# A decoder layer on eight cores: the norm factor moved to PSUM, the conv diagonals loaded instead of built, and the last tiles reordered

## Chip, cores, metric

One Trainium2 chip, eight cores; each core takes one of the eight sequences and they do not exchange data. The metric is the device time of the slowest core in microseconds (us). Most executions of a kernel agree within 0.3%. Some fall into a slower state, in which one die shows a lower clock.

Engine names in the profile: PE is TensorE (matmuls), PEld its weight loads, DVE VectorE, ACT ScalarE, POOL GpSimd, SP SyncE. SBUF is the on-chip working memory; PSUM is the small memory into which PE writes its results.

## The reference, cut

```python
def reference(x, ...):                       # x: (8, 2048, 1024)
    h = rmsnorm(x, g_mix_norm)
    proj = h @ w_in + b_in                   # q | k | v | glu | two gates
    y_attn = sliding_window_attention(q, k, v, sinks) @ w_attn_proj   # window 128
    y_conv = conformer_conv(glu_in) @ w_conv_proj + b_conv_proj       # GLU, depthwise conv 31, LayerNorm, silu
    x = x + (gate0 * y_attn + gate1 * y_conv) @ w_out
    h2 = rmsnorm(x, g_ffn_norm)
    x = x + (silu(gate) * up) @ w_ffn_down   # d_ff 2816
    return rmsnorm(x, g_final)
```

## The kernel before

The tokens of a core are treated in four groups of 512, features on the 128 partitions. A norm has four steps. Squares are formed; PE multiplies them by a matrix of 1/1024 into one PSUM bank (the statistic, already the same on all partitions); ScalarE turns that into the factor `exp(-0.5 * ln(mean + eps))`; VectorE multiplies eight tiles by gain and factor.

```python
def rstd(stat, tg):                          # norm factor of token group tg
    b = tg % 2
    act(nb.rs[:, b, :], ps[stat][:, :], AF.Ln, ..., bias=epsb)
    act(nb.rs[:, b, :], nb.rs[:, b, :], AF.Exp, ..., scale=-0.5)      # factor in SBUF

def norm_out(tg, src, c, g):                 # eight of these per group: "the body's multiplies"
    stt_("dve", hT[:, c, tsl(tg)], src[:, c, :], g[:, c:c + 1], nb.rs[:, b, :], ALU.mult, ALU.mult, ...)

def build_diag(c):                           # 16 GpSimd multiplies in all: diagonal conv weights
    for G in range(4 * c, 4 * c + 4):
        tt_("pool", wS[:, G, :, :], emask..., wcol[:, G, :]..., ALU.mult, ...)
...
for i in range(2, NTT):                      # the main loop of the first part, one step per 128 tokens
    if i < 6:
        build_diag(i - 2)
    ...
    scores(n); glu_b(tg, c); attn_t(n - 2); pv(n - 1); glu_a(tg, c)
    run(mid.get(i, ()))                      # squares, statistics, norm multiplies of later groups
    ...
    run(end.get(i, ()))
    if i in (5, 9):                          # the long steps: the q, k, v projection of group 2 or 3
        p1_qk(g, (4, 0, 1)); ...             # its matmuls read hT, which norm_out writes
```

`attn_t` issues four transposes at once on PE, once per step. They have a source line of their own, so they serve as milestones: transposes 0 to 15.

In the long step, `end` also forms the squares of group 3, and GpSimd adds them in pairs (four additions of 128x512), while VectorE multiplies group 2. At the end of the kernel the last group is treated in two halves of 256 tokens: down projection, residual addition, squares, statistics, factor, eight output multiplies, writes.

The softmax here doesn't subtract the row's maximum and nothing guards it: scores larger than these inputs give would overflow.

## Time and profile before

Median 904.51 us of six runs. The first view is the page of the slowest core (core 6): its span, busy times, the engines on the chain of work that ended last, and the group of VectorE multiplies (source line, engine, operation, output<-input, shape, count | busy us, mean ns | idle time before and who ended it).

```profile
span 902.1 us, 14231 instructions; the slowest of 8 cores (899.8 to 902.1 us)
PE 869.1 (96%) x4778; PEld 401.1 (44%) x4778; DVE 398.3 (44%) x641; ACT 323.5 (36%) x468; POOL 153.3 (17%) x173
PE 86%; DVE 3%; DMA 3%; issue 3%; POOL 2%; ACT 2%; DVEq 0%; POOLq 0%; ACTq 0%; SPq 0%
L411 DVE SCALAR_TENSOR_TENSOR arena<-arena 128x512 bf16<-128x512 f32 (+2 forms) x158 | 123.1, 814 | 115.9 <-ACT arena L398 109.0
```

PE is busy nearly always; every other engine is at or under 44%. Only what PE waits for can be gained. The next view is the same core in stretches (us from the start, length, then busy us and instruction counts by engine, clock, share of the DMA engines, GB/s).

```profile
84.00:108.00 24.00, 19.13 (x107) 8.05 (x105) 14.59 (x19) 16.17 (x23) 11.17 (x10) 0.86 0.24 57
130.00:828.00 698.00, 697.87 (x3681) 316.19 (x3672) 292.19 (x449) 212.45 (x308) 78.37 (x93) 1.00 0.31 59
880.00:902.10 22.10, 10.84 (x94) 8.71 (x92) 14.43 (x27) 9.07 (x19) 4.96 (x5) 0.84 0.52 191
```

From 130 to 828 us PE hardly ever waits (697.87 of 698 us busy). The losses are early and at the very end. The worst is the long step; here is its timeline on core 6 (start, length, engine, line, operation, count, and in brackets the idle time before it and who ended that).

```profile
83.44 0.39 PE L725 MATMUL ps<-arena 128*128 128x128 bf16 x4
...
88.52 1.02 PE L395 MATMUL ps<-arena 128*128 128x512 bf16 x4 [0.86 <-ACT arena L398]
89.06 8.72 DVE L411 SCALAR_TENSOR_TENSOR arena<-arena 128x512 bf16<-128x512 f32 x7 [0.74 <-ACT arena L398]
90.04 6.52 POOL L401 TENSOR_TENSOR arena<-arena 128x512 bf16<-128x512 f32 x4 [1.25 <-ACT arena L398]
90.56 0.81 PE L395 MATMUL ps<-arena 128*128 128x512 bf16 x3 [1.02 <-DVE arena L411]
92.23 0.89 PE L395 MATMUL ps<-arena 128*128 128x512 bf16 x3 [0.87 <-DVE arena L411]
...
108.19 0.39 PE L725 MATMUL ps<-arena 128*128 128x128 bf16 x4
```

Between transposes 5 (83.44) and 6 (108.19) PE gets three matmuls each time VectorE finishes a multiply, and waits again. Seven multiplies take 8.72 us, beside four GpSimd additions in 6.52 us (1.66 us each in the groups by form). (The step holds matmuls for 38,416 columns. The trace's matmuls of 512 columns start 0.216 us apart, which gives 16.2 us for the step; this is the "about 16" of the prediction below.) PE's waits in total, 40 to 130 us on the same core (who waited <- for whom: us, times, longest):

```profile
PE ps L395 <- DVE arena L411: 4.9, 6, 1.8
PE ps L395 <- ACT arena L398: 3.5, 8, 0.9
```

The tail, same core, from its last statistics matmuls on:

```profile
894.17 0.38 PE L395 MATMUL ps<-arena 128*128 128x256 bf16 x2 [1.80 <-ACT arena L398]
894.65 0.47 ACT L398 ACTIVATE arena<-ps,arena 128x256 f32<-128x256 f32 x1 [0.22 <-PE ps L395]
895.21 0.81 ACT L398 ACTIVATE arena<-arena 128x256 f32<-128x256 f32 x2
895.73 2.93 DVE L411 SCALAR_TENSOR_TENSOR arena<-arena 128x256 f32<-128x256 f32 x6 [1.24 <-ACT arena L398]
898.69 0.72 POOL L401 TENSOR_TENSOR arena<-arena 128x256 f32<-128x256 f32 x1 [1.50 <-ACT arena L398]
```

Ln starts 0.1 us after the last matmul; then come Exp and six multiplies on VectorE; GpSimd comes last. The span ends at 902.1, when the last write is known to have landed.

### The profile page before, as it was taken

To read this page: it belongs to the slowest core of one execution; us is meant where nothing else is said; L and a number is where in the kernel's file an instruction comes from. 1 tells how busy PE (TensorE), PEld (TensorE's weight loads), DVE (VectorE), ACT (ScalarE), POOL (GpSimd) and SP (SyncE) were. 2 spreads that over 40 slices of the span, in tenths; PEclk is the share of its full clock that TensorE was granted. 3 is DMA by queue.
4 is the path that set the end of the run, shared out by engine and by line. 5 is a ranking of instruction groups with operands and counts; after the bars stand their busy time and mean duration, and the time that the engine had idled before them with its cause. 6 is when DMAs were issued, how large, how long until landed. Compare 5 with 4: busy or idle time off the path is not lost.

```text
span 902.1 us, 14231 instructions; the slowest of 8 cores (899.8 to 902.1 us)
## 1 busy us (share of the span) xinstructions
PE 869.1 (96%) x4778; PEld 401.1 (44%) x4778; DVE 398.3 (44%) x641; ACT 323.5 (36%) x468; POOL 153.3 (17%) x173
## 2 busy tenths in 40 slices
PE   7788899999999999999999999999999999999995
PEld 4343345444444444444444444444444444444443
DVE  2257562666574334467411353121452125435346
ACT  3567656765663343243411100111001110024454
POOL 2148333321311000122000000000000000012222
PEclk9899899999999999999999999999999999999998
DMA  8750316363239632500521340212501125002115
GB/s 189 215 141 1 82 34 114 80 132 93 67 128 138 120 54 41 186 1 2 94 37 34 53 65 1 47 24 47 82 1 24 30 41 83 0 1 85 45 60 187
DMA packets 27910, 64.47 MB, mean 71 GB/s; under 512 B 3520, under 2 KB 14016, under 8 KB 27072
## 3 DMA queue, kind: packets, MB, share of 16 engines
q0 software_dynamic: 9696, 29.36, 20.2%
q1 hardware_dynamic: 17456, 33.57, 12.0%
q8 instruction: 41, 0.67, 0.3%
q10 hardware_dynamic: 688, 0.63, 0.3%
q14 instruction: 29, 0.24, 0.1%
HBM read 75.67 MB, written 8.39 MB: 93 GB/s over the span
## 4 chain that ended last, share of the span: by engine, by line
PE 86%; DVE 3%; DMA 3%; issue 3%; POOL 2%; ACT 2%; DVEq 0%; POOLq 0%; ACTq 0%; SPq 0%
PE ps L395 86%; DVE arena L411 2%; ACT arena L398 1%; POOL arena L401 1%; DMA arena<-w_qkv 1%; DMA arena<-x 1%; DMA arena<-w_glu 1%; DVE arena L401 1%; POOL arena L694 0%; PE ps L725 0%; ACT L398 0%; POOL arena L689 0%; DVE arena L716 0%; DVEq L1149 0%; SPq L388 0%
## 5 line engine op out<-in xcount | busy, mean ns | idle before, releaser
L395 PE MATMUL ps<-arena 128*128 128x512 bf16 (+5 forms) x4714 | 867.3, 364 | 24.7 <-ACT arena L398 8.7
L395 PEld LDWEIGHTS ps<-arena 128*128 128x128 bf16 (+2 forms) x4714 | 396.8, 98 | 489.0 <-issue 65.7
L401 DVE TENSOR_TENSOR arena<-arena,ps 128x512 f32<-128x512 f32 (+1 forms) x216 | 147.8, 687 | 292.3 <-PE ps L395 277.4
L398 ACT ACTIVATE arena<-ps 128x512 f32<-128x512 f32 (+1 forms) x150 | 87.8, 596 | 342.3 <-PE ps L395 336.3
L411 DVE SCALAR_TENSOR_TENSOR arena<-arena 128x512 bf16<-128x512 f32 (+2 forms) x158 | 123.1, 814 | 115.9 <-ACT arena L398 109.0
L398 ACT ACTIVATE arena<-ps,arena 128x512 f32<-128x512 f32 (+2 forms) x193 | 127.1, 683 | 123.7 <-PE ps L395 122.6
L398 ACT ACTIVATE arena<-arena 128x512 f32<-128x512 f32 (+6 forms) x98 | 78.7, 819 | 87.4 <-DVE arena L411 42.8
L401 POOL TENSOR_TENSOR arena<-arena 128x512 bf16<-128x512 f32 (+3 forms) x54 | 60.7, 1128 | 200.8 <-ACT arena L398 190.8
L388 POOL DMA_DIRECT2D arena<-w_ffn_in x22 | 11.7, 533 | 347.2 <-PE ps L395 347.2
L401 DVE TENSOR_TENSOR arena<-arena 128x512 f32<-128x512 f32 (+3 forms) x75 | 53.1, 737 | 8.6 <-ACT arena L398 3.3
L398 ACT ACT_TABLE_LOAD x27 | 34.6, 1283 | 21.7 <-PE ps L395 11.1
L401 DVE TENSOR_TENSOR arena<-ps,arena 128x256 bf16<-128x256 f32 (+3 forms) x72 | 22.6, 333 | 28.3 <-PE ps L395 24.3
L411 DVE SCALAR_TENSOR_TENSOR arena<-arena,ps 128x512 f32<-128x512 f32 x32 | 21.9, 685 | 18.2 <-ACT arena L398 16.8
L411 DVE SCALAR_TENSOR_TENSOR arena<-ps,arena 128x512 f32<-128x512 f32 x32 | 21.7, 685 | 17.2 <-PE ps L395 17.2
L689 POOL TENSOR_SCALAR_AFFINE_SELECT arena<-arena 128x1024 bf16<-128x1024 bf16 x16 | 18.6, 1165 | 51.2 <-ACT arena L398 51.2
L407 POOL TENSOR_SCALAR arena<-arena 128x512 f32<-128x512 f32 x16 | 15.6, 983 | 56.6 <-ACT arena L398 55.5
L694 POOL TENSOR_SCALAR_AFFINE_SELECT arena<-arena 128x1024 bf16<-128x1024 bf16 x15 | 18.3, 1222 | 0.7
L753 POOL CAST arena<-arena 128x512 bf16<-128x512 f32 x16 | 12.2, 766 | 34.6 <-ACT arena L398 25.9
L729 DVE COPY arena<-ps 128x512 bf16<-128x512 bf16 x16 | 6.7, 419 | 15.3 <-PE ps L725 15.3
L388 POOL DMA_DIRECT2D arena<-w_mix x8 | 4.4, 556 | 25.6 <-PE ps L395 25.3
L716 DVE RECIPROCAL arena<-arena 128x4 f32<-128x4 f32 x32 | 5.7, 178 | 3.3
L725 PE MATMUL ps<-arena 128*128 128x128 bf16 x64 | 6.2, 219 | 0.7 <-ACT arena L398 0.7
(18 smaller groups left out, 20.9 us busy)
## 6 DMA issues: line engine op xcount, KB each, us to landing
arena<-x SPq DMA_DIRECT2D x32, 512.0 KB, 6.8
arena<-w_ffn_in POOLq DMA_DIRECT2D x22, 512.0 KB, 5.3
arena<-arena SPq DMA_DIRECT2D x128, 67.5 KB, 2.0
arena<-w_mix POOLq DMA_DIRECT2D x8, 768.0 KB, 13.0
out<-arena SPq DMA_DIRECT2D x6, 1024.0 KB, 3.9
arena<-w_ffn_down POOLq DMA_DIRECT2D x2, 1536.0 KB, 15.0
arena<-w_ffn_down POOLq DMA_DIRECT2D x2, 1280.0 KB, 13.6
arena<-w_glu POOLq DMA_DIRECT2D x4, 512.0 KB, 9.9
```

Of the source, the lines that this page charges most:

```text
L388: return S.add(eng, lambda e: e.dma_start(out=out, in_=in_, **kw), r=r, w=w, dma=True)
L395: return op("pe", lambda e: e.matmul(out=out, lhsT=lhsT, rhs=rhs, start=start, stop=stop, **kw), r, w)
L398: return op("act", lambda e: e.activation(out=out, in_=in_, func=func, **kw), r, w)
L401: return op(eng, lambda e: e.tensor_tensor(out=out, in0=in0, in1=in1, op=alu), r, w)
L407: return op(eng, lambda e: e.tensor_scalar(out=out, in0=in0, scalar1=s1, scalar2=s2, op0=op0, op1=op1), r, w)
L411: return op(eng, lambda e: e.scalar_tensor_tensor(out=out, in0=in0, scalar=scalar, in1=in1, op0=op0, op1=op1), r, w)
L689: op("pool", lambda e, pw=pw: e.affine_select(out=pw, in_=pw, pattern=[[0, 8], [1, 128]], compare_op=ALU.is_ge, fill=0.0, base=0, channel_ ...
L694: op("pool", lambda e, pw=pw: e.affine_select(out=pw, in_=pw, pattern=[[0, 8], [-1, 128]], compare_op=ALU.is_gt, fill=0.0, base=0, channel ...
L716: op("dve", lambda e, dg=dg: e.reciprocal(out=dg, in_=dg), r=[dres], w=[dres])
L725: op("pe", lambda e, c=c: e.transpose(out=ps_bf[bank][:, c * 128:(c + 1) * 128], in_=attn_tm[:, b, c * 128:(c + 1) * 128], identity=ident) ...
L729: op("dve", lambda e: e.tensor_copy(out=attnT[:, :, n * 128:(n + 1) * 128], in_=ps_bf[bank][:, 0:512].rearrange("p (c j) -> p c j", c=4)), ...
L753: op("pool", lambda e: e.tensor_copy(out=ybf[tg][c], in_=y), r=[yr], w=["ybf.%d" % c])
```

## The change

The intent has three parts. (1) The norm factor is written to PSUM, over its own statistic, so that the VectorE multiply has one SBUF input and one PSUM input. (2) The diagonal conv weights are laid out on the host and loaded by one 2 MB transfer, instead of 16 GpSimd multiplies; the factor 0.5 that was in the diagonals goes into the scale of the two ScalarE evictions. (3) The tail is rewritten: squares and statistics are interleaved with the tiles of both halves, gains for GpSimd's tiles are prepared early, the last half's output is split three to GpSimd and five to VectorE, and the factor is formed twice, in PSUM for VectorE and in SBUF for GpSimd.

```diff
     def rstd(stat, tg):
-        act(nb.rs[:, b, :], nb.rs[:, b, :], AF.Exp, ..., scale=-0.5)
+        act(ps[stat][:, :], nb.rs[:, b, :], AF.Exp, ..., scale=-0.5)
+        rs_bank[b] = stat
     def norm_out(tg, src, c, g):
-        stt_("dve", hT[...], src[:, c, :], g[:, c:c + 1], nb.rs[:, b, :], ALU.mult, ALU.mult, ...)
+        stt_("dve", hT[...], src[:, c, :], g[:, c:c + 1], ps[rs_bank[b]][:, :], ALU.mult, ALU.mult, ...)
...
-        if i < 6:
-            build_diag(i - 2)
+        if i == 4:
+            dma("pool", wS..., wdiag_d..., w=["wS"])
...
-        act(y, ps[bank][:, :], AF.Identity, ..., bias=conv_b[:, c:c + 1])
+        act(y, ps[bank][:, :], AF.Identity, ..., scale=0.5, bias=conv_b[:, c:c + 1])
...
     def rstd_seg(stat, b, n):
         act(nb.rs[:, b, 0:n], ps[stat][:, 0:n], AF.Ln, ...)
+        act(ps[stat][:, 0:n], nb.rs[:, b, 0:n], AF.Exp, ...)
         act(nb.rs[:, b, 0:n], nb.rs[:, b, 0:n], AF.Exp, ...)
...
-                    down_final(wb, nf, tg, 0, 256, 0, False)
-                    down_final(wb, nf, tg, 256, 256, 1, True)
+                    down_tail(wb, nf, tg)
...
+    def down_tail(wb, nf, tg):               # cut: tile(half, c) = down projection, addition, squares
+        ...
+        tile(1, 2)
+        pes.pop(0)()                         # statistics matmuls of an earlier tile
+        rstd_seg(segs[0][1], 0, 256)
+        final_pre(tg, 0, 256, 3)             # gain multiply on ScalarE, for GpSimd's tiles
+        final_pre(tg, 0, 256, 7)
+        ...
+        tile(1, 6)
+        for k in (3, 5, 7):
+            final_pre(tg, 256, 256, k)
+        while pes:
+            pes.pop(0)()
+        rstd_seg(segs[1][1], 1, 256)
+        ...                                  # rest of half 0 on VectorE, then half 1: three GpSimd, five VectorE
```

More of the change, by code (lines that the diff above doesn't have):

```diff
@@ L215, in build_program @@
     vec_d = din("vecs", [128, NV])
-    wcol_d = din("wcol", [128, 16, 8])
+    wdiag_d = din("wdiag", [128, 16, 8, 32])
     out_d = nc.dram_tensor("out", [NTG, 128, 8, 512], F32, kind="ExternalOutput").ap()
@@ L240, in build_program @@
     ONES_OFF = region(512)
-    EM_OFF = region(64)
-    WCOL_OFF = region(512)
     ESINK_OFF = region(32)
@@ L261, in build_program @@
     ones = A.bf16(ONES_OFF, 256).rearrange("p (w m) -> p w m", w=2)
-    emask = A.bf16(EM_OFF, 32)
-    wcol = A.f32(WCOL_OFF, 128).rearrange("p (g m) -> p g m", g=16)
     esink = A.f32(ESINK_OFF, 8)
@@ L520, in rstd @@
         act(nb.rs[:, b, :], ps[stat][:, :], AF.Ln, r=[P(stat), "epsb"], w=["rs%d" % b], bias=epsb)
-        act(nb.rs[:, b, :], nb.rs[:, b, :], AF.Exp, r=["rs%d" % b], w=["rs%d" % b], scale=-0.5)
+        act(ps[stat][:, :], nb.rs[:, b, :], AF.Exp, r=["rs%d" % b], w=["rs%d" % b, P(stat)], scale=-0.5)
+        rs_bank[b] = stat
+    rs_bank = {}
     def norm_out(tg, src, c, g):
         b = tg % 2
-        stt_("dve", hT[:, c, tsl(tg)], src[:, c, :], g[:, c:c + 1], nb.rs[:, b, :], ALU.mult, ALU.mult,
-             r=["x.%d.%d" % (tg, c), "rs%d" % b, "vec"], w=["hT.%d.%d" % (tg, c)])
+        stt_("dve", hT[:, c, tsl(tg)], src[:, c, :], g[:, c:c + 1], ps[rs_bank[b]][:, :], ALU.mult, ALU.mult,
+             r=["x.%d.%d" % (tg, c), P(rs_bank[b]), "vec"], w=["hT.%d.%d" % (tg, c)])
     def fm_matmuls(w, wres, tg, bank):
@@ L604, in late_consts @@
         ts_("pool", hln, vec[:, 34:42], 0.5, None, ALU.mult, None, r=["vec"], w=["hln"])
-        tt_("dve", emask, ident[:, 0:32], ident[:, 32:64], ALU.add, r=["ident"], w=["emask"])
-        tt_("dve", emask, emask, ident[:, 64:96], ALU.add, r=["ident", "emask"], w=["emask"])
-        tt_("dve", emask, emask, ident[:, 96:128], ALU.add, r=["ident", "emask"], w=["emask"])
-        ts_("dve", emask, emask, 0.5, None, ALU.mult, None, r=["emask"], w=["emask"])
     for n in range(NTT):
@@ L641, in build_program @@
     SCALE = HD ** -0.5
-    def build_diag(c):
-        for G in range(4 * c, 4 * c + 4):
-            tt_("pool", wS[:, G, :, :], emask.unsqueeze(1).broadcast_to([128, 8, 32]),
-                wcol[:, G, :].unsqueeze(2).broadcast_to([128, 8, 32]), ALU.mult,
-                r=["emask", "wcol"], w=["wS"])
     def fill_zs(tg, half):
@@ L749, in conv_unit @@
         M.claim("ybf.%d" % c, ybfoff[tg][c], 1024)
-        act(y, ps[bank][:, :], AF.Identity, r=[P(bank), "vec"], w=[yr], bias=conv_b[:, c:c + 1])
+        act(y, ps[bank][:, :], AF.Identity, r=[P(bank), "vec"], w=[yr], scale=0.5, bias=conv_b[:, c:c + 1])
         act(ysq[tg][c], ps[bank][:, :], AF.Square, r=[P(bank), "vec"], w=["ysq.%d" % c],
-            bias=conv_b[:, c:c + 1])
+            scale=0.5, bias=conv_b[:, c:c + 1])
         op("pool", lambda e: e.tensor_copy(out=ybf[tg][c], in_=y), r=[yr], w=["ybf.%d" % c])
@@ L836, in build_program @@
     load_glu(1)
-    dma("sp", wcol, wcol_d, w=["wcol"])
     claim_x((2,), lambda g: 0)
@@ L871, in build_program @@
         n = i + 2
-        if i < 6:
-            build_diag(i - 2)
+        if i == 4:
+            dma("pool", wS.rearrange("p g m c -> p (g m c)"), wdiag_d.rearrange("p g m c -> p (g m c)"), w=["wS"])
         if i == 6:
@@ L1048, in rstd_seg, with final_pre, final, put_out @@
         act(nb.rs[:, b, 0:n], ps[stat][:, 0:n], AF.Ln, r=[P(stat), "epsb"], w=["rs%d" % b], bias=epsb)
+        act(ps[stat][:, 0:n], nb.rs[:, b, 0:n], AF.Exp, r=["rs%d" % b], w=[P(stat)], scale=-0.5)
         act(nb.rs[:, b, 0:n], nb.rs[:, b, 0:n], AF.Exp, r=["rs%d" % b], w=["rs%d" % b], scale=-0.5)
-    def final(tg, lo, n, b, k, last):
+        fin_bank[b] = stat
+    fin_bank = {}
+    def final_pre(tg, lo, n, k):
         xr = xf(tg, lo, k)
         xs = xt[:, tg, k, lo:lo + n]
-        if k in (3, 7):
-            act(xs, xs, AF.Copy, r=[xr, "vec"], w=[xr], scale=g_fin[:, k:k + 1])
+        act(xs, xs, AF.Copy, r=[xr, "vec"], w=[xr], scale=g_fin[:, k:k + 1])
+    def final(tg, lo, n, b, k, pool):
+        xr = xf(tg, lo, k)
+        xs = xt[:, tg, k, lo:lo + n]
+        if pool:
             tt_("pool", xs, xs, nb.rs[:, b, 0:n], ALU.mult, r=[xr, "rs%d" % b], w=[xr])
         else:
-            stt_("dve", xs, xs, g_fin[:, k:k + 1], nb.rs[:, b, 0:n], ALU.mult, ALU.mult,
-                 r=[xr, "rs%d" % b, "vec"], w=[xr])
-        w = 2 if last else 4
-        if k in ((1, 2, 5, 6) if last else (2, 6)):
-            k0 = k // w * w
-            on = "out.%d.%d.%d" % (tg, k, lo)
-            dma("act" if last and k in (2, 5) else "sp", out_d[tg, :, k0:k0 + w, lo:lo + n],
-                xt[:, tg, k0:k0 + w, lo:lo + n], r=[xf(tg, lo, j) for j in range(k0, k0 + w)], w=[on])
-            outs.append(on)
+            stt_("dve", xs, xs, g_fin[:, k:k + 1], ps[fin_bank[b]][:, 0:n], ALU.mult, ALU.mult,
+                 r=[xr, P(fin_bank[b]), "vec"], w=[xr])
+    def put_out(eng, tg, lo, n, k0, w):
+        on = "out.%d.%d.%d" % (tg, k0, lo)
+        dma(eng, out_d[tg, :, k0:k0 + w, lo:lo + n], xt[:, tg, k0:k0 + w, lo:lo + n],
+            r=[xf(tg, lo, j) for j in range(k0, k0 + w)], w=[on])
+        outs.append(on)
     outs = []
@@ L1095, in ff_down, with down_final, fin @@
             r=[P(bank)] + xr, w=[xf(tg, lo, k) for k in range(c, c + m)] if fin else xr)
-    def down_final(wb, nf, tg, lo, n, b, last):
+    def down_final(wb, nf, tg, b):
         stat = st_rot()
-        m = 512 // n
-        for c in range(0, 8, m):
-            ff_down(wb, nf, tg, lo, n, c, True)
-            clock[0] += 1
-            if m > 1 or c % 2 == 1:
-                c0, w = (c, m) if m > 1 else (c - 1, 2)
-                later(2 if m > 1 else 4, sq_seg(stat, tg, lo, n, c0, w) if m > 1 else sq_seg_sum(stat, tg, c0))
-                if c0 + w == 8:
-                    later(2, lambda: rstd_seg(stat, b, n))
-                    later(3, *[lambda k=k: final(tg, lo, n, b, k, last) for k in (3, 0, 1, 2, 7, 4, 5, 6)])
-            tick(2 * m)
+        def fin(k):
+            if k in (3, 7):
+                final_pre(tg, 0, 512, k)
+            final(tg, 0, 512, b, k, k in (3, 7))
+            if k in (2, 6):
+                put_out("sp", tg, 0, 512, k - 2, 4)
+        for c in range(8):
+            ff_down(wb, nf, tg, 0, 512, c, True)
+            clock[0] += 1
+            if c % 2 == 1:
+                later(4, sq_seg_sum(stat, tg, c - 1))
+                if c == 7:
+                    later(2, lambda: rstd_seg(stat, b, 512))
+                    later(3, *[lambda k=k: fin(k) for k in (3, 0, 1, 2, 7, 4, 5, 6)])
+            tick(2)
@@ new lines, in down_tail, with tile @@
+    def down_tail(wb, nf, tg):
+        segs = [(0, st_rot(), 0), (256, st_rot(), 1)]
+        pes = []
+        def tile(s, c):
+            lo, stat, b = segs[s]
+            ff_down(wb, nf, tg, lo, 256, c, True)
+            pes.append(sq_seg(stat, tg, lo, 256, c, 2))
+        for c in (0, 2, 4, 6):
+            tile(0, c)
+            tick(2)
+            if c >= 4:
+                pes.pop(0)()
+        drain0 = len(bg)
+        tile(1, 0)
+        drain()
+        pes.pop(0)()
+        tile(1, 2)
+        pes.pop(0)()
+        rstd_seg(segs[0][1], 0, 256)
+        final_pre(tg, 0, 256, 3)
+        final_pre(tg, 0, 256, 7)
+        final(tg, 0, 256, 0, 3, True)
+        final(tg, 0, 256, 0, 7, True)
+        tile(1, 4)
+        pes.pop(0)()
+        final(tg, 0, 256, 0, 0, False)
+        final(tg, 0, 256, 0, 1, False)
+        put_out("sp", tg, 0, 256, 0, 2)
+        tile(1, 6)
+        for k in (3, 5, 7):
+            final_pre(tg, 256, 256, k)
+        while pes:
+            pes.pop(0)()
+        rstd_seg(segs[1][1], 1, 256)
+        final(tg, 0, 256, 0, 2, False)
+        put_out("sp", tg, 0, 256, 2, 2)
+        for k in (4, 5, 6):
+            final(tg, 0, 256, 0, k, False)
+        put_out("sp", tg, 0, 256, 4, 4)
+        for k in (3, 5, 7):
+            final(tg, 256, 256, 1, k, True)
+        for k in (0, 1, 2, 4, 6):
+            final(tg, 256, 256, 1, k, False)
+        put_out("sp", tg, 256, 256, 0, 2)
+        put_out("act", tg, 256, 256, 2, 2)
+        put_out("sp", tg, 256, 256, 4, 2)
+        put_out("act", tg, 256, 256, 6, 2)
@@ L1137, in build_program @@
                     ff_in(0, fglob, TGO[ti + 1])
-                    down_final(wb, nf, tg, 0, 512, ti % 2, False)
+                    down_final(wb, nf, tg, ti % 2)
                     for fi in range(1, nf):
@@ L1192, in make_in_maps @@
     w32 = np.concatenate([np.zeros((1, CC), np.float32), f["conv_w"].reshape(CW, CC)], axis=0)
-    wcol = w32.reshape(8, 4, 16, 32).transpose(1, 3, 2, 0).reshape(128, 16, 8)
+    wcol = w32.reshape(8, 4, 16, 32).transpose(1, 3, 2, 0)
+    wdiag = np.zeros((4, 32, 16, 8, 32), np.float32)
+    for i in range(32):
+        wdiag[:, i, :, :, i] = wcol[:, i]
     shared = {
@@ L1197, in make_in_maps @@
         "w_ffn_in": w_fi, "w_ffn_down": f["w_ffn_down"].reshape(NFF, 128, 1024),
-        "vecs": vecs, "wcol": wcol,
+        "vecs": vecs, "wdiag": wdiag.reshape(128, 16, 8, 32),
     }
```

## The prediction

> **What bounds it.** The page shows PE busy 869.1 of 902.1 us; by stretches PE is 100% busy from 140 to 830 us, and the chain of waits is 86% PE. What does not touch the stretches 44-128 us and 828-902 us is worth nothing.
>
> **Where PE starves (core 6).**
> - Around 50 us: PE waits 1.8 us for a normalising VectorE multiply (scalar_tensor_tensor).
> - 84-100 us, the worst. Timed by the four-transpose groups of the timeline, the loop step with the next query/key projection takes 83.44 to 108.19 = 24.7 us. Its matmuls at 0.213 us per 512 columns need about 16 (estimate), so 8.8 us are lost. The multiplies that feed it (seven in 8.72 us, up to 1.57 us each) meet GpSimd additions running up to 1.7 us. Undisturbed, that multiply takes 0.69 us. On two of the three other cores that I read the PE clock did not dip here, yet the step took about as long: the wait is the cause, the dip mostly a consequence.
> - 111-122 us: multiplies of 1.1 us beside GpSimd masks; about 1 us lost.
> - Tail: PE waits 0.92, 0.32 and 1.8 us for squares; after the last matmul (894.55) come Ln, Exp, six multiplies, a late ACT copy and a GpSimd multiply to 899.4, then the write until 902.1.
>
> **What the change does.**
> 1. The norm factor goes to PSUM. The Trainium skill ("SBUF — State Buffer", Who interferes with whom) says that a VectorE instruction with at most one SBUF input, outside the 2-port modes, does not contend with GpSimd. This trace agrees: forms with one PSUM input average 0.685-0.687 us (216 of them), the all-SBUF multiply 0.871. I expect the 64 early multiplies at 0.69. The FFN norms (450 us) are hidden by PE: no gain.
> 2. Diagonal conv weights come by DMA. This removes 16 GpSimd multiplies (12.6 us busy, of which only part blocks: the steps at 66-76 us already take 4.81 us against an estimated PE minimum of 4.9), four 0.17 us VectorE operations and a 64 KB load. It adds one 2 MB load at about 73 us, where the DMA timeline is empty (68-90 us). From 1.5 MB in 15.0 us I estimate 20 us to landing, needed at about 118 us: hidden.
> 3. The 0.5 moves into the eviction scale: free.
> 4. The tail interleaves squares, statistics and output multiplies, prepares gains early and splits the last half three for GpSimd, five for VectorE.
>
> **Gain on the critical path (estimates).** About 1.5 us at 50 us; about 5 at 84-108 (multiplies 0.69 instead of about 1.45, six to seven of them; but GpSimd's four additions, 1.27 us each, then end later than they do, and ScalarE's table loads at 81-89 us stay); 1 at 111-122; 2 in the tail (1.2 of PE waits, about 1 after the last Exp, less the second Exp, 0.42). Sum about 9.5 us: **895.0 us**, range 890.5 to 899.5. Faster by over 2% (below 886.4): 0.03; within 2%: 0.96; slower: 0.01.
>
> **What would show it.**
> - Early multiplies at 0.69 us beside GpSimd; no GpSimd 128x256 multiplies.
> - The long step at about 20 us instead of 24.7; PE's wait for VectorE multiplies in 40-130 us falls from 4.9 to under 2.
> - The stretch 130-828 us keeps its length.
> - From PE's last matmul to the end about 6.3 us instead of 7.5.
> - Output writes land 2.4 us after issue, as before.
>
> **What would make it wrong.** ScalarE, busy 24.2 of 30 us in 60-90, may be the next limit of the long step, so that only 2-3 us come there. The additions on GpSimd may replace the multiplies as PE's wait. The 2 MB load may delay the conv shift copies that start at 92 us. Or the freed GpSimd brings masks earlier and more than 10 us come back.

## The result

The changed kernel takes 894.64 us (median of eight runs, two of them slow; 904.6 us for the kernel before in the same sessions, three of 16 slow). The ratio is 0.989, 95% interval 0.9879 to 0.990. A ratio here is the mean time of one kernel's fast runs over that of the other's in the same rounds, so it is not quite the ratio of the quoted medians. The medians count slow runs too, here and below; without them none would be more than 0.4 us lower. The output is correct.

The page of the slowest core after (core 2), the same lines as before:

```profile
span 892.8 us, 14120 instructions; the slowest of 8 cores (890.7 to 892.8 us)
PE 857.3 (96%) x4692; PEld 400.3 (45%) x4778; DVE 379.5 (43%) x636; ACT 325.4 (36%) x474; POOL 136.7 (15%) x159
PE 90%; DMA 3%; ACT 2%; issue 2%; DVE 1%; POOL 0%; SPq 0%; POOLq 0%; ACTq 0%; DVEq 0%
L407 DVE SCALAR_TENSOR_TENSOR arena<-arena,ps 128x512 bf16<-128x512 f32 (+2 forms) x125 | 83.1, 702 | 50.7 <-ACT ps L394 32.8
```

The multiplies now read `arena,ps`, and VectorE's share of the chain fell from 3% to 1%. (A few matmul records are missing on this core, so its PE count and PE busy time are not compared.) The same stretches, on core 6 as before, each moved by what had been gained up to there:

```profile
81.00:101.00 20.00, 17.26 (x125) 8.43 (x124) 9.82 (x19) 17.07 (x24) 7.92 (x7) 1.00 0.22 50
122.00:820.00 698.00, 697.87 (x3670) 316.40 (x3669) 290.33 (x450) 212.58 (x309) 79.34 (x93) 1.00 0.31 60
871.00:891.80 20.80, 10.55 (x92) 8.57 (x90) 12.55 (x24) 9.64 (x21) 4.78 (x6) 0.82 0.55 202
```

The middle is the same to the last digit shown (PE busy 697.87 of 698 us). The long step on core 6:

```profile
81.02 0.39 PE L714 MATMUL ps<-arena 128*128 128x128 bf16 x4
...
86.64 0.69 DVE L407 SCALAR_TENSOR_TENSOR arena<-arena 128x512 bf16<-128x512 f32 x1 [1.46 <-ACT arena L394]
87.24 4.04 DVE L407 SCALAR_TENSOR_TENSOR arena<-arena,ps 128x512 bf16<-128x512 f32 x6
87.62 5.08 POOL L397 TENSOR_TENSOR arena<-arena 128x512 bf16<-128x512 f32 x4 [2.09 <-ACT arena L394]
88.13 12.70 PE L391 MATMUL ps<-arena 128*128 128x512 bf16 x82 [1.02 <-DVE arena L407]
...
100.67 0.39 PE L714 MATMUL ps<-arena 128*128 128x128 bf16 x4
```

The six norm multiplies take 4.04 us and the four additions beside them 5.08 us (1.27 us each): both became faster at once. After one wait of 1.02 us PE runs through. The step takes 19.65 us instead of 24.75. PE's wait for VectorE multiplies in 40 to 130 us fell from 4.9 to 1.3 us on this core.

The tail on core 6, whose last matmul ends at 883.54:

```profile
880.76 3.45 ACT L394 ACTIVATE arena<-arena 128x256 f32<-128x256 f32 x8
882.64 0.90 PE L391 MATMUL ps<-arena 128*128 128x256 bf16 x4 [1.60 <-ACT arena L394]
884.12 0.45 ACT L394 ACTIVATE arena<-ps,arena 128x256 f32<-128x256 f32 x1
884.66 0.39 ACT L394 ACTIVATE ps<-arena 128x256 f32<-128x256 f32 x1
885.15 2.05 DVE L407 SCALAR_TENSOR_TENSOR arena<-arena,ps 128x256 f32<-128x256 f32 x5 [1.34 <-ACT ps L394]
885.70 2.09 POOL L397 TENSOR_TENSOR arena<-arena 128x256 f32<-128x256 f32 x3 [2.56 <-ACT arena L394]
```

VectorE and GpSimd end within 0.6 us of each other, nearly together, as meant. But Ln (884.12) starts 0.58 us after the last matmul instead of 0.1, because ScalarE works without a pause until 884.2: five gain multiplies stand in its queue among the squares.

The whole account, medians over the eight cores, in us. "First GLU matmul" is the first one after the wait for the GLU weights.

| stretch | before | after |
|---|---|---|
| start to first GLU matmul (loads) | 32.35 | 32.63 |
| first GLU matmul to transposes 0 | 22.97 | 19.98 |
| transposes 0 to 5 | 27.94 | 27.95 |
| transposes 5 to 6 (the long step) | 23.72 | 19.65 |
| transposes 6 to 10 | 35.26 | 33.62 |
| transposes 10 to the last Silu | 734.69 | 734.60 |
| last Silu to last matmul | 16.41 | 14.62 |
| last matmul to end of computation | 4.87 | 4.25 |
| end of computation to end | 2.71 | 3.82 |

Four stretches gain 10.5 us between them, the end of computation comes 0.6 us closer to the last matmul, and the final writes give back 1.1. That last figure is of these two profiles alone: in the other profiles of the same new tail (experiments 3, 4, 7, 10 and 11) the last line of the table is 3.2 to 4.3, in those of the old tail (experiments 1, 2 and 5) 2.6 to 2.9.

Part of this is clock. The trace's clock records show PE at half rate in stretches of 3.4 or 6.8 us. Before, three of the eight cores had one near 50 us and four had one near 90 us (one core had both); after, none had one near 50 and two had one near 88 us. The long step without such a dip takes 23.6 us before and 19.65 after. With one it takes 24.7 on three cores and 23.84 on the fourth before, and 21.15 after. So the dip costs 0.2 to 1.5 us where it occurs, and the wait itself 4 us.

### The profile page after: what moved, and what is told of

It reads as the page before. It is cut to its first block, busy times and chain, and to the rows that moved or that the text cites. A ratio compares the mean times of both kernels' runs of the same rounds, so it can differ in the third digit from the quotient of the medians.

```text
span 892.8 us, 14120 instructions; the slowest of 8 cores (890.7 to 892.8 us)
## 1 busy us (share of the span) xinstructions
PE 857.3 (96%) x4692; PEld 400.3 (45%) x4778; DVE 379.5 (43%) x636; ACT 325.4 (36%) x474; POOL 136.7 (15%) x159
## 4 chain that ended last, share of the span: by engine, by line
PE 90%; DMA 3%; ACT 2%; issue 2%; DVE 1%; POOL 0%; SPq 0%; POOLq 0%; ACTq 0%; DVEq 0%
PE ps L391 90%; ACT arena L394 1%; DMA arena<-w_qkv 1%; DMA arena<-w_glu 1%; DMA arena<-x 1%; DVE arena L407 1%; POOL arena L397 0%; ACT L394 0%; DVE arena L397 0%; PE ps L714 0%; ACT ps L394 0%; SPq L384 0%; POOLq L1199 0%; ACTq L152 0%; POOL arena L384 0%
## 5 line engine op out<-in xcount | busy, mean ns | idle before, releaser
L391 PE MATMUL ps<-arena 128*128 128x512 bf16 (+5 forms) x4628 | 855.7, 362 | 26.2 <-ACT arena L394 8.5
L407 DVE SCALAR_TENSOR_TENSOR arena<-arena,ps 128x512 bf16<-128x512 f32 (+2 forms) x125 | 83.1, 702 | 50.7 <-ACT ps L394 32.8
L394 ACT ACTIVATE arena<-arena 128x512 f32<-128x512 f32 (+5 forms) x91 | 73.8, 832 | 81.2 <-DVE arena L407 39.3
L407 DVE SCALAR_TENSOR_TENSOR arena<-arena 128x512 bf16<-128x512 f32 (+1 forms) x64 | 45.7, 721 | 84.5 <-ACT arena L394 77.7
L397 POOL TENSOR_TENSOR arena<-arena 128x512 bf16<-128x512 f32 (+2 forms) x39 | 46.6, 1200 | 196.5 <-ACT arena L394 182.8
L397 DVE TENSOR_TENSOR arena<-arena 128x512 f32<-128x512 f32 (+2 forms) x72 | 50.7, 734 | 11.2 <-ACT arena L394 3.3
L678 POOL TENSOR_SCALAR_AFFINE_SELECT arena<-arena 128x1024 bf16<-128x1024 bf16 x16 | 17.6, 1103 | 60.7 <-ACT arena L394 60.7
L683 POOL TENSOR_SCALAR_AFFINE_SELECT arena<-arena 128x1024 bf16<-128x1024 bf16 x15 | 16.4, 1092 | 1.5 <-ACT arena L394 0.4
L394 ACT ACTIVATE ps<-arena 128x512 f32<-128x512 f32 (+1 forms) x13 | 7.4, 569 | 1.2
## 6 DMA issues: line engine op xcount, KB each, us to landing
arena<-w_mix POOLq DMA_DIRECT2D x8, 768.0 KB, 12.6
```

The costliest lines, as they stand in the source:

```text
L391: return op("pe", lambda e: e.matmul(out=out, lhsT=lhsT, rhs=rhs, start=start, stop=stop, **kw), r, w)
L394: return op("act", lambda e: e.activation(out=out, in_=in_, func=func, **kw), r, w)
L397: return op(eng, lambda e: e.tensor_tensor(out=out, in0=in0, in1=in1, op=alu), r, w)
L407: return op(eng, lambda e: e.scalar_tensor_tensor(out=out, in0=in0, scalar=scalar, in1=in1, op0=op0, op1=op1), r, w)
L678: op("pool", lambda e, pw=pw: e.affine_select(out=pw, in_=pw, pattern=[[0, 8], [1, 128]], compare_op=ALU.is_ge, fill=0.0, base=0, channel_ ...
L683: op("pool", lambda e, pw=pw: e.affine_select(out=pw, in_=pw, pattern=[[0, 8], [-1, 128]], compare_op=ALU.is_gt, fill=0.0, base=0, channel ...
```

## The experiments

**Theory A**: the multiply with two SBUF inputs and a running GpSimd operation block each other; PE waited for that; moving one input to PSUM ends it. The Trainium skill says this of the hardware ("SBUF — State Buffer", SBUF: two separate sides, and Who interferes with whom): the second SBUF read interface of VectorE is shared with GpSimd, and one of the two blocks fully. The trace before agrees so far as it shows multiplies up to 1.76 us beside additions of 1.66 us, against 0.69 and 1.27 us undisturbed. A multiply and an addition together take 1.68 us there. In the trace after, where neither blocks the other, multiplies start 0.66 us apart and additions 1.24 to 1.33, about 1.9 together; so the two nearly take turns, with some overlap. **Rival B**: the gain comes from GpSimd's freed time, since 16 multiplies left it. The first four runs separate the parts, all timed against the kernel before in the same rounds.

### 1. The body's factor in PSUM, nothing else

```diff
-        act(nb.rs[:, b, :], nb.rs[:, b, :], AF.Exp, ...)
+        act(ps[stat][:, :], nb.rs[:, b, :], AF.Exp, ...)      # and norm_out reads ps[rs_bank[b]]
```

> The kernel before with one part of the change: the norm factor of the two norms in the body goes to PSUM. Theory A (the two-SBUF-input multiply and GpSimd block each other, and that wait was PE's): the 64 body multiplies run at 0.69 to 0.75 us although GpSimd still builds the diagonals, the long step (transposes 5 to 6) falls from 23.9 to 20 or 20.5 us, the stretch from the first GLU matmul to the first transposes falls by 2.5 to 3 us, and the whole kernel is 6 to 8 us faster. Rival B (the gain is GpSimd's freed time, from the diagonals leaving it): under 2 us faster, long step still above 22.5 us.

Measured: 897.29 us, ratio 0.9915 (0.9902 to 0.9929): 7.7 us of the change's gain. First GLU matmul to transposes 0: 19.83 us. The long step: 19.6 us on three cores; 21.2 on five with a half-rate stretch near 87 us, so its median is 21.1, above the range that I gave. The multiplies of the norm take 0.73 to 0.75 us, all 64 of them on every core, although GpSimd still builds the diagonals. The view of the slowest core, 40 to 130 us (count, then shortest, median and longest in ns, first and last start):

```profile
L411 DVE SCALAR_TENSOR_TENSOR arena<-arena,ps x24: 739/742/748, 44.1 to 113.7; 128x512 bf16<-128x512 f32 x24
```

Theory A holds and B fails.

### 2. The diagonals by transfer, nothing else

```diff
-        if i < 6:
-            build_diag(i - 2)
+        if i == 4:
+            dma("pool", wS..., wdiag_d..., w=["wS"])
```

> The kernel before with only the diagonals by DMA (and 0.5 in the eviction). Theory A: nothing on the chain needed that GpSimd time; 0 to 1.5 us faster, the long step falls by at most 1.5 us, the four steps between transposes 1 and 5 keep their lengths to 0.1 us. Rival B: 4 us faster or more, long step at 20 us.

Measured: 904.22 us, ratio 0.9991 (0.9978 to 1.0005); the interval includes no gain. The long step takes 23.62 us, transposes 1 to 5 are unchanged (21.87 us), and the seven multiplies and four GpSimd additions take as long as before (on the slowest core 8.73 and 6.54 us):

```profile
90.55 8.73 DVE L407 SCALAR_TENSOR_TENSOR arena<-arena 128x512 bf16<-128x512 f32 x7 [1.42 <-ACT arena L394]
```

Removing 12.6 us of GpSimd work bought nothing measurable.

### 3. The tail, nothing else

```diff
-                    down_final(wb, nf, tg, 0, 256, 0, False)
-                    down_final(wb, nf, tg, 256, 256, 1, True)
+                    down_tail(wb, nf, tg)     # with the final factor in PSUM
```

> The kernel before with only the new tail and the final norm's factor in PSUM. The body keeps its length; from the last Silu to the last matmul 14.6 us instead of 16.4; from the last matmul to the end about 7.9 instead of 7.6 us; in all 1.5 us faster (0.5 to 2.5).

Measured: 902.84 us, ratio 0.9981 (0.9967 to 0.9995), 1.7 us. Last Silu to last matmul 14.63, as expected; then 4.25 to the end of computation and 3.28 to the end, together 7.5 where 7.9 was expected. The three parts alone give 0.0085, 0.0009 and 0.0019; their sum, 0.0113, agrees with the whole change's 0.0110.

### 4. The change without the body's factor in PSUM

```diff
-        act(ps[stat][:, :], nb.rs[:, b, :], AF.Exp, ...)
+        act(nb.rs[:, b, :], nb.rs[:, b, :], AF.Exp, ...)
```

> The changed kernel with the body's norm factor back in SBUF. Theory A: it loses 5 to 8 us of the 10 us gain (about 900 to 902 us); the body multiplies beside GpSimd additions take 1.3 us or more again; the half-rate clock stretches of 3.4 or 6.8 us near 50 and 90 us come back on some of the cores. Rival B: it loses under 3 us.

Measured: 902.45 us, ratio 0.9974 (0.9959 to 0.9989). Undoing this one part loses 8 of the 10 us. The long step is back at 23.68 us, the longest early multiply at 1.77, and half-rate stretches are back on two cores near 50 us and on four near 90.

### 5. A factor in SBUF beside a quiet GpSimd

Experiment 1 shows that PSUM helps, not why. Here the factor stays in SBUF, and the GpSimd additions of the long step go instead; the diagonals are loaded, as in experiment 2.

```diff
-            if tg >= 3:
-                pes.append(sq_sum(...))       # squares added in pairs by GpSimd
-            else:
-                pes.append(sq_mm(...))
+            pes.append(sq_mm(...))            # PE sums all eight squares: four more matmuls
```

> The factor stays in SBUF, diagonals by DMA, and the four GpSimd additions of the third norm's statistics are gone (PE sums all eight squares instead: four more matmuls in the long step, 0.85 us). If theory A's mechanism is blocking by a running GpSimd operation, the six multiplies of the long step run at 0.69 to 0.75 us from SBUF, and the step takes 20.0 to 21.0 us. If a factor in SBUF is slow by itself, they stay at 1.3 us or more and the step above 23 us. The stretch to the first transposes, whose blocking comes from masks and is untouched, stays at 22 to 23.5 us.

Measured: 900.59 us, ratio 0.9971 (0.9954 to 0.9987). In the timeline of core 6:

```profile
88.46 4.67 DVE L407 SCALAR_TENSOR_TENSOR arena<-arena 128x512 bf16<-128x512 f32 x7 [1.42 <-ACT arena L394]
89.96 11.62 PE L391 MATMUL ps<-arena 128*128 128x512 bf16 x78 [1.02 <-DVE arena L407]
```

The same seven multiplies, from SBUF, take 4.67 us instead of 8.73 (experiment 2, which differs from this only in the additions), and the long step takes 20.41 us, of which 0.86 are the added matmuls by estimate (four at the trace's 0.216). (Two cores had a half-rate stretch near 90 us and took 22.0.) The stretch to transposes 0 has a median of 21.9 us, a little below the range given for it, and half-rate stretches near 50 us remain there on three cores. A factor in SBUF is not slow; it is slow beside GpSimd. This is the mechanism of theory A.

### 6. The gain multiplies taken off ScalarE's busiest moment

```diff
+        final_pre(tg, 0, 256, 3)              # half 0: before tile(1, 2), in an idle gap
+        final_pre(tg, 0, 256, 7)
         tile(1, 2)
...
-        for k in (3, 5, 7):
-            final_pre(tg, 256, 256, k)
         while pes:
             pes.pop(0)()
         rstd_seg(segs[1][1], 1, 256)
+        for k in (3, 5, 7):                   # half 1: after Ln and Exp
+            final_pre(tg, 256, 256, k)
```

> The changed kernel, with ScalarE's five gain multiplies taken off the way of the last square and the last Ln. Computation from the last Silu to its end: 0.5 to 0.9 us shorter. If the end waits for the last half's factor, the end comes 0.5 to 0.9 us sooner too; if the output writes have become the limit (they landed 3 to 5 us after issue instead of 2.4), the gap from the last computation to the end grows by most of what the computation saves.

Measured: ratio 0.9892 (0.9876 to 0.9909), as the change. The last four writes start 2.16 us after the last matmul instead of 2.62 (2.19 before the change), so the gains were what delayed them. But last Silu to end of computation fell only from 18.87 to 18.71 us: a miss. The last lines of core 6 of this kernel, whose last matmul ends at 881.35:

```profile
881.45 0.47 ACT L394 ACTIVATE arena<-ps,arena 128x256 f32<-128x256 f32 x1 [0.62 <-PE ps L391]
882.51 2.05 DVE L407 SCALAR_TENSOR_TENSOR arena<-arena,ps 128x256 f32<-128x256 f32 x5 [0.83 <-ACT ps L394]
883.45 2.09 POOL L397 TENSOR_TENSOR arena<-arena 128x256 f32<-128x256 f32 x3 [2.86 <-ACT arena L394]
```

Ln is 0.1 us behind the matmul again, and VectorE starts 1.16 us after it instead of 1.61. But GpSimd, which now waits for the gains behind the factor, starts 2.10 us after it (2.16 in the change) and ends last. The wait moved to another engine's queue. The end, in one profile each, came 3.57 us after the computation (3.82 in the change); the same tail in experiments 8 and 12 gave 3.04 and 2.90, so one profile says little here, and the runs do not tell whether writes or GpSimd would be the next limit.

### 7. The third group's norm one loop step earlier

```diff
-    mid = {3: sqs2, 4: [stats2] + norms2[:2], 5: norms2[2:5], ...}
-    end = {5: norms2[5:] + sqs3}
+    mid = {2: sqs2, 3: [stats2] + norms2[:2], 4: norms2[2:5], 5: norms2[5:], ...}
+    end = {5: sqs3}
```

> The changed kernel, with the third group's squares, statistics and multiplies one loop step earlier, so that the projection in the long step finds them done. If what is left of the long step (19.65 us against an estimated 16) is the wait for the multiplies, behind ScalarE's table loads, the stretch from transposes 1 to 6 (41.5 us) falls by 1 to 2.5 us. If ScalarE as a whole is the limit, it falls by under 0.5 us.

Measured: ratio 0.9891 (0.9872 to 0.9911), no gain. The long step fell to 17.51 us, but transposes 1 to 4 rose from 14.26 to 17.06; transposes 1 to 6 take 41.81 us instead of 41.53. PE's waits on core 1 of this kernel, 40 to 130 us:

```profile
PE ps L391 <- ACT arena L394: 3.9, 8, 1.0
PE ps L391 <- POOL arena L397: 1.1, 2, 0.8
PE ps L391 <- DVE arena L407: 0.3, 1, 0.3
```

The wait for VectorE is nearly gone (1.3 to 0.3) and GpSimd's additions take its place (0 to 1.1); the wait for ScalarE stays (3.8 to 3.9). So what is left of this part's loss is not where one norm stands. That ScalarE as a whole is the limit fits these lines, but no run removed ScalarE work, so this stays argued.

### 8. Experiments 6 and 7 together

> Both edits together: 1 to 3 us faster than the changed kernel, 892 to 893.5 us; the savings of the two add.

Measured: 893.32 us, ratio 0.9887 (0.9872 to 0.9902). This is no clear gain over the change: the median lies in the range given, but the kernel before was faster in these rounds too (903.22 us), and the ratio is that of the change within its interval.

### 9. Fewer writes in the tail (wrong output on purpose)

```diff
-        put_out("sp", tg, 0, 256, 2, 2)
-        put_out("sp", tg, 0, 256, 4, 4)
```

> Wrong on purpose: the changed kernel without two of the first half's three output writes in the tail (768 KB of the last 2 MB). If the last writes land late (3 to 4 us after issue) because they queue behind the first half's, they land in 2.2 to 2.6 us here, and the gap from the last computation to the end is 2.3 to 2.8 us instead of 3.2 to 4.3. If their lateness has another cause (two issuing queues, four issues within 2 us), it stays above 3.2 us. Computation in the tail keeps its length.

Its output is wrong, which doesn't matter for the time. Over all cores the last four writes land 2.64 us after issue (median), against 3.31 in the changed kernel and 2.47 in the kernel before. The end follows the computation by 3.16 us, against 3.82 and 2.71. The gap did not fall to 2.3 to 2.8 as expected of a full explanation. Nor is queueing behind the first half's writes shown for a part of it. The same tail with all its writes was profiled in experiments 3, 4, 7, 10 and 11 too: there the last four land after 2.83, 3.42, 2.76, 2.75 and 3.15 us, and the end follows after 3.28, 4.26, 3.22, 3.24 and 3.62. Without two writes it is hardly better than experiments 7 and 10 are with them, and the spread between profiles of one tail is larger than the difference in question. The cores do lie close together here (3.10 to 3.33 us), while with all writes some reach 4 us and more, so the writes may explain the excess of single profiles; one look does not settle it. Why this tail has at least 3.2 us in every profile, where the old one has 2.6 to 2.9, stays open. The last four writes are issued within 1.7 us in the new tail and 2.8 in the old, so they may delay each other. Two lines each show the tail's issues on core 6 (count, KB each, us to landing), first of the changed kernel, then of this one:

```profile
out<-arena SPq DMA_DIRECT2D x4, 256.0 KB, 3.3
out<-arena ACTq DMA_DIRECT2D x2, 256.0 KB, 3.6
```

```profile
out<-arena SPq DMA_DIRECT2D x3, 256.0 KB, 2.2
out<-arena ACTq DMA_DIRECT2D x2, 256.0 KB, 2.7
```

### 10. The clock kept up in an earlier wait

In the profiles before and after the change every core runs at half clock for 3.4 or 6.8 us from about 29 to 34 us on, during or just after PE's wait for the first GLU weights. The Trainium skill ("TensorE: Matmul & The Clock Gate", What's actually happening) says that the clock is set in windows of 3.4 us by how busy PE was; the lengths in the records, 3.4 and 6.8 us, agree. Here dummy matmuls into the free statistics bank fill that wait.

```diff
     run(sqs)
+    warm_st(32)                               # 32 dummy matmuls of 256 columns into ps[7]
     glu_b(0, 0)
```

> The changed kernel with 32 dummy matmuls (about 3.4 us at full clock) in PE's wait for the first GLU weights, which is followed by 3.4 or 6.8 us at half clock on nearly all cores. If the half clock there costs PE time on the chain, those stretches go on most cores, the first GLU matmul to first transposes falls from 19.8 to 17.5 or 18.5 us, and the kernel is 1 to 2 us faster than the changed one (893 us). If the weights and ScalarE set the pace there, under 0.5 us.

### 11 and 12. The changed kernel again, and 6, 7 and 10 together

> The changed kernel itself, unaltered, in the same rounds, as the yardstick: 893.5 to 895.5 us, ratio to the kernel before 0.988 to 0.990.

> Tail gains off the path, third group's norm one step earlier and the clock kept up, together: 1 to 2.5 us faster than the changed kernel of the same rounds, nearly all of it from the clock.

Measured in the same rounds: the changed kernel 895.7 us, ratio 0.9897 (0.9881 to 0.9914); experiment 10 893.41 us, 0.9868 (0.9853 to 0.9883); all three 893.45 us, 0.9862 (0.9846 to 0.9878). Core 3 of the changed kernel, then of experiment 10, at the first GLU matmuls:

```profile
33.92 9.78 PE L391 MATMUL ps<-arena 128*128 128x512 bf16 x44 [5.07 <-DMA arena<-w_glu]
```

```profile
34.22 7.96 PE L391 MATMUL ps<-arena 128*128 128x512 bf16 x44 [1.48 <-DMA arena<-w_glu]
```

The weights come no sooner (33.92 and 34.22), but PE has waited 1.48 us instead of 5.07, and the same 44 matmuls then take 7.96 us instead of 9.78. No core has a half-rate stretch near 31 us any more. On some cores PE now has no gap there, so I cannot take the stretch from the first GLU matmul as a milestone; the median time of transposes 0 from the start is 51.6 us, against 53.7 in experiment 11. That pair alone shows little, for the same start without dummies gave 51.9, 51.9 and 52.4 in experiments 6, 8 and 9, as the weights came at other times. The landing of the first GLU weights is a milestone that all cores have. From it to transposes 0 it takes 18.28 us here in the median (one core 20.88, the others 18.27 to 18.43) and 20.02 in experiment 11. Two cores of experiment 7 had no half-rate stretch there without any dummies, and they took 18.26 too; cores with one took 19.6 to 21.2 in the kernels with this start and no dummies. So it is the half rate that costs, and by this milestone the expected 17.5 to 18.5 us are met. Experiment 10 is 2.3 us faster than the changed kernel in the medians; the two intervals barely overlap. It beats both kernels. All three edits together add nothing visible to it. (The changed kernel's 895.7 us lie just above the range given for them; its ratio lies inside.)

Two further builds meant to form the factor in a single operation (a power on VectorE, a reciprocal root on ScalarE) did not compile and were not run.

## Why the prediction was right, and where its steps were not

- **The total**: 895.0 predicted, 894.64 measured, inside the range. The step of the argument that carried it, that the two-SBUF-input multiply beside GpSimd is what PE waits for, is shown by experiments 1, 4 and 5.
- **Around 50 us**: 1.5 predicted, 3.0 measured (22.97 to 19.98). The term was mis-sized. It took only the wait of 1.8 us; on three cores that wait was also followed by 3.4 us at half clock, which went with it. The wait itself was sized well: from the landing of the first GLU weights to transposes 0, cores without any half-rate stretch there take 20.0 to 20.2 us with the factor in SBUF (one core each in experiments 3, 4 and 5) and 18.3 in PSUM (experiments 7 and 8).
- **The long step**: "about 20 us instead of 24.7" on core 6; measured 19.65 from 24.75. PE's wait for multiplies went to 1.3 us, under 2 as said. But core 6 was one of the cores with a dip: over the cores the step gained 4.1 us (23.72 to 19.65) and not the 5 of the sum. The cores without a dip had not taken "about as long"; they took 23.6. The "up to 1.57 us each" of the prediction is the longest multiply near 50 us; in the long step it is 1.76. The multiplies with the factor in PSUM take 0.74 us each by the record and not 0.69, the same whatever GpSimd does.
- **111 to 122 us**: 1 predicted; transposes 6 to 8 gained 1.1, and 8 to 10 another 0.5.
- **The diagonals**: predicted hidden, and hidden (experiment 2). Their load landed in 8.3 to 10.3 us over the cores, not in the 20 that I had scaled from another load; it did not matter.
- **The middle**: unchanged, as said.
- **The tail**: 2 predicted. The computation gained 2.4 (last Silu to end of computation, 21.27 to 18.87), but the end only 1.3 (24.0 to 22.7). The step that failed is "From PE's last matmul to the end about 6.3 us instead of 7.5": it is 8.1 (4.25 and 3.82), and 7.5 to 8.5 in the other profiles of this tail. Two things were missed. The gain multiplies sit on ScalarE before the last Ln and delay the last four writes by 0.4 us (experiment 6), and the writes, "2.4 us after issue, as before", land after 3.3 (2.8 to 3.4 in the other profiles of this tail). Why they do is open (experiment 9). The extra gain at 50 us covered this and the long step's missing 1 us. That was luck: the total is nearer than its parts.
- **The clock**: "the dip mostly a consequence" holds near 50 us, where the dips went with the wait. Near 90 it holds in part: two of eight cores still dipped after the change, and five in experiment 1, where the multiplies were as fast, though for 3.4 us and no longer for 6.8. And a dip has its own price, 0.2 to 1.5 us in the long step, and experiment 10 shows one that could be removed at its cause.

## What to carry to other kernels

When a two-input VectorE operation on the critical path runs beside GpSimd, compare its longest record with its shortest before blaming its size: putting one input in PSUM (ScalarE can write it there) was worth more here than taking work off GpSimd. In a tail, first ask when the last writes can be issued, and measure how long they take to land in more than one profile; shortening the arithmetic before them paid only in part here. And look at what PE does in the microseconds after each of its waits, since a wait can cost its length once and then a clock step.

## What the Trainium skill lacked or had wrong

- "SBUF — State Buffer", Who interferes with whom: it names `tensor_tensor` with two SBUF inputs as contending with GpSimd; it does not name `scalar_tensor_tensor` with a pointer scalar. The runs show that it contends as well (up to 1.76 us instead of 0.69 beside GpSimd additions), that the GpSimd side also lengthens (1.66 instead of 1.27 us), and that one SBUF and one PSUM input removes it (0.73 to 0.75 us in every run with the factor in PSUM). The page's rule itself agrees with every run here.
- "TensorE: Matmul & The Clock Gate", Why this matters for your kernels: it advises no idle gaps over about 3 us. That is not enough. Before the change, cores went to half clock after 3.4 us windows in which the longest PE gap was 1.02 us (near 90 us, PE busy 45% by the records) or 1.8 us (near 50 us, 42 to 43%). The page's own section on a second failure mode describes such micro-idling without a number for the busy share.
- No page that I read says how much of a half-clock stretch is hidden when PE waits on other engines anyway. Here stretches of 3.4 or 6.8 us cost 0.2 to 1.5 us in the long step (before and after the change), and 1.3 to 2.9 us near 31 us (19.6 to 21.2 against 18.3, experiment 10).
